# Spreading the DRAM weight sums of a hybrid encoder over the program: one transfer every 11 ticks, group by group

## The chip, the cores and the metric

One core of a Trainium2 chip runs one program. The metric is the device time of one execution in microseconds (us). The engines are TensorE (PE, with its weight loads PEld), VectorE (DVE), ScalarE (ACT), GpSimd (POOL) and SyncE (SP). DMA transfers are issued from SP's, ACT's and POOL's queues and moved by 16 DMA engines. All data are float32.

## The reference, cut to what matters

One layer over 2048 positions of width 1024. It is a mixer with two branches followed by a gated feed-forward network:

```python
xn = rmsnorm(x, norm1_g)
z = xn @ w_in                                   # 1024 -> 4608 columns
u_pool, zq, zf, zi, zo, zg = split(z)
gates = sigmoid(zg + b_gate)                    # two branches of 1024
ya = pool_mixer(u_pool, pool_w, pool_scale) @ w_pa     # trailing means, windows 2, 4, 8, 16
yb = hgrn2_mixer(zq, zf, zi, zo, lb, norm_g) @ w_pb    # gated recurrence, 4 heads
x = x + (gates[0] * ya + gates[1] * yb) @ w_o
h = causal_conv3(rmsnorm(x, norm2_g) @ w_up) + conv_b  # 1024 -> 5632
val, gate = split(h)
x = x + (silu(gate) * val) @ w_down                    # 2816 -> 1024
out = rmsnorm(x, final_g)
```

## The kernel before, in words

**Passes and stages.** The program runs twice over its weights, each time for two blocks of 512 positions (1024 in all). Each pass has these stages: `io` (the recurrence's input and output-gate columns), the projection (14 units of the other columns of `w_in`), the two branch products `pa` and `pb`, the output projection `wo`, the up-projection `up` (22 units with convolution and gate) and the down-projection `dn`.

**Seven products in place of eight.** The large products use a Strassen-type scheme (Winograd's form). A 2 by 2 block product is made of seven block products, called P1 to P7 here (M1 to M7 for `wo` and `dn`), for which sums of weight blocks and sums of input blocks are needed. For a pair of weight tiles with four quarters, the four sums are s1, s2, s3 and s4: s1 = q2 + q3, s3 = q2 + q0, s2 = s1 + q0 and s4 = s2 + q1. P5 uses s1, P6 uses s2, P7 uses s3, P3 uses s4; P1, P2 and P4 use plain quarters.

**Two float32r halves.** Each operand is split into a high part (a cast on ACT, line 207 for weights) and a low part (a subtraction on DVE, line 208). Every block product is three matmuls: high by high, high by low, low by high.

**The weight stream.** The class `Stream` holds the whole program's list of weight operands in order. A raw tile of 128 by 512 is loaded through SP's queue (line 185) up to 8 tiles ahead (`N_RAW`), and an operand is converted up to 4 ahead of the one in use (`LOOKAHEAD`, 6 buffers).

**Ticks.** Every sixth matmul of the helper `mm` is a tick (`MM_PER_TICK = 6`). At a tick the stream converts at most one operand, and every live task is stepped whose wait, in ticks, is over. A unit of seven products has 84 matmuls, 14 ticks; one operand lasts two ticks. Matmuls of the recurrence aren't counted.

**Where the weight sums come from.** The up-projection's sums are made in DRAM and are used in both passes. The second pass takes those of `io` and of the projection from DRAM as well. The first pass makes its own `io` and projection sums as it goes, on POOL (lines 311 and 369; some of `io`'s on DVE). The sums in DRAM are made in groups of mostly four units: six groups for `up` (tiles `su0` to `su5`), one for `io` (`so0`) and four for the projection (`si0` to `si3`: the forget and query columns, gates 0 to 3, the pool columns with two units, gates 4 to 7). A group takes eight transfers, each of 1 MB (512 KB for a group of two): four plain copies issued on ACT (line 263) and four that add to what lies in DRAM, issued on POOL (line 260, `accum_op`). In each group the order is: s1 = q2, s3 = q2, s1 += q3, s3 += q0, s2 = s1, s2 += q0, s4 = s2, s4 += q1. That makes 11 groups, 88 transfers.

**When they are issued before.** `Sums.make` starts a task that issues one transfer and then waits `SUM_LAG = 4` ticks. It goes through the eight steps in the outer loop and through the groups in the inner one. The `up` task starts when the first `io` stage is done (line 1103): 48 transfers in 192 ticks. The `io` and projection tasks start together at the first up-projection (lines 1373 and 1374): 8 transfers in 32 ticks beside 32 in 128. A load that needs a sum finishes the whole task first (`join` in `of`).

**The scheduler's freedom.** The program is given to a scheduler that orders each engine's instructions by a simulated timeline. A copy on ACT is tied behind the stream's latest cast (`issue_after(stream.mark.ins)`), so it isn't placed ahead of the tick at which it is issued. An accumulation on POOL has no such tie, only its dependence on the transfer whose result it adds to.

The task's heart, lines 252 to 264:

```python
for dst, src, add in (("s1", 2, 0), ("s3", 2, 0), ("s1", 3, 1), ("s3", 0, 1),
                      ("s2", "s1", 0), ("s2", 0, 1), ("s4", "s2", 0), ("s4", 1, 1)):
    for g in range(n):
        ...
        yield SUM_LAG
```

Of the kernel before, what the change touches and what calls it, by code (L numbers as in the profile page):

```python
# [11 lines left out]
F32 = mybir.dt.float32  # L12
# [3 lines left out]
ALU = mybir.AluOpType  # L16
AX = mybir.AxisListType

P = 128
# [52 lines left out]
FIN_WAIT = 4  # L72
N_RAW = 8
GROUP = 4
SUM_LAG = 4
N_OPS = 6
LOOKAHEAD = 4
MM_PER_TICK = 6
# [3 lines left out]
def tile_trunk(  # L82
# [16 lines left out]
    pe, act, dve, pool, sp = nc.tensor, nc.scalar, nc.vector, nc.gpsimd, nc.sync  # L99
# [6 lines left out]
    dram = ctx.enter_context(tc.tile_pool(name="dram", bufs=1, space=bass.MemoryType.DRAM))  # L106
# [15 lines left out]
    class Task:  # L122
        def __init__(self, gen):
            self.gen = gen
            self.wait = 0
            self.live = True
            tasks.append(self)
# [15 lines left out]
    def join(task):  # L143
        while task.live:
            task.step()
# [86 lines left out]
    stream = Stream()  # L232

    class Sums:


        def __init__(self, name, groups):

            self.name, self.groups = name, groups
            self.where = {}  # L240
            self.task = None
            for g, (units, _) in enumerate(groups):
                for i, u in enumerate(units):
                    self.where[u] = g, i
            self.t = {}

        def make(self):
            def gen():
                n = len(self.groups)
                for g, (units, _) in enumerate(self.groups):  # L250
                    for k in ("s1", "s2", "s3", "s4"):
                        nm = f"{self.name}{g}{k}"
                        self.t[g, k] = dram.tile([P, len(units), 512], F32, tag=nm, name=nm)
                for dst, src, add in (("s1", 2, 0), ("s3", 2, 0), ("s1", 3, 1), ("s3", 0, 1),
                                      ("s2", "s1", 0), ("s2", 0, 1), ("s4", "s2", 0),
                                      ("s4", 1, 1)):
                    for g in range(n):
                        x = self.t[g, src] if isinstance(src, str) else self.groups[g][1][src]
                        if add:
                            pool.dma_start(self.t[g, dst], x, accum_op=ALU.add)  # L260
                        else:
                            with tc.issue_after(stream.mark.ins):
                                act.dma_start(self.t[g, dst], x)
                        yield SUM_LAG

            self.task = Task(gen())

        def of(self, unit, key):
            def src():
                join(self.task)  # L270
                g, i = self.where[unit]
                return self.t[g, key][:, i, :]
            return src

    def grouped(src, mv, mg, names):
        n = len(names)

        def part(m, c):
            m0, st = m[0], m[1] - m[0]
            v = src[m0 : m0 + st * (n - 1) + 1 : st].rearrange("m p c -> p m c")  # L280
            return v[:, :, c * 512 : (c + 1) * 512]

        return names, [part(mv, 0), part(mv, 1), part(mg, 0), part(mg, 1)]
# [54 lines left out]
    def proj_tiles(kind, i):  # L338
        if kind == "fq":
            return C_F // P + i, C_Q // P + i  # L340
        if kind == "u":
            return 2 * i, 2 * i + 1
        return C_G // P + i, C_G // P + KD + i
# [91 lines left out]
    sums = {}  # L435
# [6 lines left out]
    def group_in(kind, i0, n):  # L442
        mv, mg = zip(*(proj_tiles(kind, i) for i in range(i0, i0 + n + 1)))
        return grouped(w_in_t, mv, mg, [(kind, i) for i in range(i0, i0 + n)])

    io_q = w_io.rearrange("k p c -> p k c")
    sums["up"] = Sums("su", [group_up(m0) for m0 in range(0, MF, GROUP)])
    sums["io"] = Sums("so", [(list(range(4)),
                              [io_q[:, :, c * 512 : (c + 1) * 512] for c in (0, 3, 1, 2)])])
    sums["in"] = Sums("si", [group_in(*g) for g in (("fq", 0, 4), ("g", 0, 4), ("u", 0, 2),  # L450
                                                    ("g", 4, 4))])

# [642 lines left out]
    def mixer(b0, forms, late):  # L1095
# [4 lines left out]
        md, od, gd = {}, {}, {}  # L1100
        proj_io(b0, forms, late, vd, zd)
        if b0 == 0:
            sums["up"].make()


        queue = []
# [171 lines left out]
    def ffn(b0, forms, late):  # L1278
# [90 lines left out]
                gs[k, hf] = fetch(gd[k, hf], f"g{b0}_{k}_{hf}")  # L1369
            return gs[k, hf]  # L1370

        if not b0:
            sums["io"].make()
            sums["in"].make()
        down = Rows(f"dn{b0}", "dn", DOWN, MF // 2, get_g, acc, 5)
        EARLY = {"P7": 2, "P4": 3}
        units = {}
# [63 lines left out]
    for b in range(0, SEQ // TB, 2):  # L1441
        forms, task, late = nxt
        join(task)
        forms, task, late = mixer(b, forms, late)
        join(task)
        nxt = ffn(b, forms, late)
# [47 lines left out]
```

## Time and profile before

| what | value |
|---|---|
| time, median of 3 runs | 2718.53 us (2715.54 to 2718.91) |
| the profiled execution's own time | 2723.21 us |
| its span, first to last instruction | 2721.5 us |
| mean granted TensorE clock | 0.979 |
| busy share PE, DVE, ACT, POOL | 94%, 80%, 43%, 41% |
| moved by DMA | 467.50 MB, mean 172 GB/s |
| of these by POOL's queue (q0) | 41.95 MB, 21184 packets |
| of these by ACT's queue (q10) | 67.23 MB, 25264 packets |

How to read it: the page is one execution. A queue's bytes include reads and writes of stores and fetches that have nothing to do with sums, on ACT's queue above all. Busy time of an engine is given as a share of the span, or of a stretch where a row names one. A row of the chain of waits has its start, its length and what ran or was waited for. In rows of instructions, a line number is that of the kernel, then come the operation, output and inputs by the program's names with the buffer numbers left out, the count, and the time. A waiting row reads "engine, what waited, what it waited for: us in total, times, longest".

### The profile page before, as it was taken

The page shows a single profiled execution, that of the slowest core. Times are in us where ns is not written, and L with a number is a line of the kernel's source. Part 1 is how long each engine was busy: PE and PEld are TensorE (multiplying, and loading weights), DVE is VectorE, ACT ScalarE, POOL GpSimd, SP SyncE. Part 2 cuts the span into 40 slices and gives each one's busy share as a digit, 9 for nine tenths or more (in the row PEclk, how much of TensorE's full clock was granted, in tenths as well). Part 3 has the DMA queues.
Part 4 walks back from the last instruction along what each step waited for, and adds up shares of the span by engine and source line. Part 5 has one row for each costly group of instructions (what it writes and reads, how often), then busy time and mean ns, then how long its engine had stood idle before and what let it go on. Part 6 is the DMA issues. An engine that isn't in the chain of part 4 may idle for free.

```text
span 2721.5 us, 35290 instructions
## 1 busy us (share of the span) xinstructions
PE 2571.2 (94%) x11464; PEld 2072.5 (76%) x11464; DVE 2190.7 (80%) x3414; ACT 1166.9 (43%) x2204; POOL 1113.3 (41%) x1171
## 2 busy tenths in 40 slices
PE   7989998999799999989999999999999999998898
PEld 6777777887578888767878788888777888885686
DVE  7879779579687777799987777674898777778998
ACT  5324333423454444443364344342345544444344
POOL 5544344076442111197761111211853211117785
PEclk9999999999899999999999999999999999999999
DMA  6797569654999543474465344347443433436552
GB/s 213 216 265 194 153 192 236 212 192 153 284 262 284 165 127 118 143 262 132 159 198 159 97 124 128 113 150 246 164 146 94 126 121 123 121 123 227 196 168 85
DMA packets 254472, 467.50 MB, mean 172 GB/s; under 512 B 24688, under 2 KB 41200, under 8 KB 253936
## 3 DMA queue, kind: packets, MB, share of 16 engines
q1 hardware_dynamic: 207840, 356.08, 41.1%
q0 software_dynamic: 21184, 41.95, 8.7%
q10 hardware_dynamic: 25264, 67.23, 6.6%
q8 instruction: 90, 1.47, 0.2%
q14 instruction: 94, 0.77, 0.1%
HBM read 391.75 MB, written 157.29 MB: 202 GB/s over the span
## 4 chain that ended last, share of the span: by engine, by line
PE 60%; DVE 16%; DMA 7%; issue 5%; POOL 5%; ACT 2%; SPq 0%; ACTq 0%; DVEq 0%; POOLq 0%
PE up_Z L148 13%; PE up_X L148 8%; PE up_V L148 8%; DVE ops L208 5%; PE gr_Z L148 4%; PE pa L148 3%; PE pb L148 3%; PE gr_X L148 2%; PE gr_V L148 2%; PE dn_M L148 2%; PE fr_Z L148 2%; DMA g<-dg 1%; PE fr_X L148 1%; PE io_Z L148 1%; DMA su3s<-in_w_up_t 1%
## 5 line engine op out<-in xcount | busy, mean ns | idle before, releaser
L207 ACT CAST ops<-raw 128x512 fp32r<-128x512 f32 x582 | 358.5, 620 | 716.2 <-PE up_Z L148 240.0
L208 DVE TENSOR_TENSOR ops<-raw,ops 128x512 fp32r<-128x512 f32 x582 | 450.7, 780 | 124.1 <-ACT ops L207 119.1
L1296 POOL COPY hist<-h 128x2 f32<-128x2 f32 x88 | 38.3, 435 | 403.5 <-DVE h L942 402.9
L1301 DVE SCALAR_TENSOR_TENSOR e<-h,cols,e 128x512 f32<-128x512 f32 x176 | 136.3, 794 | 18.8 <-ACT e L1299 13.8
L1299 ACT ACTIVATE e<-h,cols 128x512 f32<-128x512 f32 x176 | 138.1, 812 | 19.0 <-DVE h L940 11.7
L1303 DVE SCALAR_TENSOR_TENSOR e<-h,cols,e 128x512 f32<-128x512 f32 x176 | 136.0, 777 | 1.3
L1294 POOL COPY h<-h 128x2 f32<-128x2 f32 x88 | 38.0, 458 | 152.1 <-DVE h L940 148.6
L1232 POOL TENSOR_TENSOR ya<-ya,gl 128x512 f32<-128x512 f32 x32 | 47.2, 1486 | 106.8 <-DVE gl L1231 106.8
L979 DVE TENSOR_TENSOR up_u<-up_Z,up_e 128x512 f32<-128x512 f32 x44 | 30.4, 690 | 66.8 <-PE up_Z L148 64.9
L1134 POOL TENSOR_TENSOR q<-q,qs 128x512 f32<-128x512 f32 x16 | 23.3, 1456 | 131.9 <-ACT qs L1133 94.1
L1307 ACT ACTIVATE e<-e 128x512 f32<-128x512 f32 x88 | 55.3, 629 | 40.6 <-DVE e L1303 40.6
L809 POOL COPY qm<-q 128x64 f32<-128x64 f32 x64 | 25.8, 457 | 109.5 <-DVE q L874 21.6
L1171 ACT ACTIVATE gt<-gt,cols 128x512 f32<-128x512 f32 x48 | 34.8, 726 | 74.0 <-DVE gt L942 58.0
L1038 DVE TENSOR_TENSOR ac<-ac,dn_M 128x512 f32<-128x512 f32 x96 | 59.9, 679 | 3.6 <-PE dn_M L148 3.6
L1038 DVE TENSOR_TENSOR x<-x,wo_M 128x512 f32<-128x512 f32 x96 | 61.1, 678 | 0.4
L940 DVE TENSOR_TENSOR h<-up_Z,up_e 128x512 f32<-128x512 f32 x44 | 30.4, 691 | 38.1 <-PE up_Z L148 38.0
L942 DVE TENSOR_TENSOR h<-up_u,up_V 128x512 f32<-128x512 f32 x88 | 60.0, 682 | 0.1
L817 PE MATMUL pl<-qm,k 128*128 128x192 f32 x256 | 48.7, 332 | 8.0 <-DVE f L835 3.1
L817 PEld LDWEIGHTS pl<-qm,k 128*128 128x128 f32 x256 | 43.1, 191 | 13.1 <-issue 4.6
L148 PE MATMUL dn_M<-ops,dn_M_0h 128*128 128x512 f32 x112 | 39.3, 425 | 13.9 <-DVE ops L208 5.5
L1294 POOL COPY h<-hist 128x2 f32<-128x2 f32 x88 | 52.2, 642 | 0.0
L1308 DVE TENSOR_TENSOR e<-e,e 128x512 f32<-128x512 f32 x72 | 51.6, 717 | 0.4
(1743 smaller groups left out, 9025.4 us busy)
## 6 DMA issues: line engine op xcount, KB each, us to landing
raw<-in_w_dn SPq DMA_DIRECT2D x198, 256.0 KB, 3.6
raw<-in_w_up_t SPq DMA_DIRECT2D x132, 256.0 KB, 3.2
raw<-in_w_in_t SPq DMA_DIRECT2D x98, 256.0 KB, 3.6
dg<-e SPq DMA_DIRECT2D x88, 256.0 KB, 3.5
g<-dg SPq DMA_DIRECT2D x88, 256.0 KB, 5.3
raw<-in_w_o SPq DMA_DIRECT2D x80, 256.0 KB, 3.6
raw<-in_w_io SPq DMA_DIRECT2D x68, 256.0 KB, 4.9
x<-in_x SPq DMA_DIRECT2D x64, 256.0 KB, 5.3
```

What stands on the lines that cost most here:

```text
L148: pe.matmul(*args, **kw)
L207: self.mark = act.copy(hi, v)
L208: dve.tensor_tensor(lo, v, f32(hi), ALU.subtract)
L817: pe.matmul(pa_[:, c * 192 : c * 192 + 192], ks[:, (i + c) * P : (i + c + 1) * P], mv[:, c].rearrange("p s x -> p (s x)"), start=True, sto ...
L942: dve.tensor_tensor(dst, t, ps, ALU.add if how == "add" else ALU.subtract)
L1038: dve.tensor_tensor(t, t, ps[pr[0], j], ALU.add if sg > 0 else ALU.subtract)
L1294: pool.tensor_copy(h[:, 0:2], hist[:, mt] if hf == 0 else hs[s, 0][:, TB : TB + 2])
L1299: act.activation(t, h[:, 2:], AF.Identity, bias=col(o_cb + mt), scale=col(o_cw + 4 * MF + mt))
L1301: dve.scalar_tensor_tensor(t, h[:, 1 : 1 + TB], col(o_cw + 2 * MF + mt), t, ALU.mult, ALU.add)
L1303: dve.scalar_tensor_tensor(t, h[:, 0:TB], col(o_cw + mt), t, ALU.mult, ALU.add)
L1307: act.activation(g, g, AF.Silu)
L1308: (pool if m < G_POOL else dve).tensor_tensor(g, g, ts[0, hf], ALU.mult)
```

## The change

One task makes all the sums, for `up`, then `io`, then the projection, group after group in the order in which they are used. Each group's eight transfers come one after another, 11 ticks apart (`SUM_LAG = 11`). The task starts where the `up` task started, after the first `io` stage. A load that needs a sum steps the task until that sum's group is done, rather than finishing all of it. The number of transfers, their sizes, their engines and what they compute stay.

```diff
-SUM_LAG = 4
+SUM_LAG = 11
...
-            self.task = None
+            self.done = set()
...
-        def make(self):
-            def gen():
-                n = len(self.groups)
...
-                    for g in range(n):
-                        x = self.t[g, src] if isinstance(src, str) else self.groups[g][1][src]
...
-            self.task = Task(gen())
+        def make(self, g):
+            n = len(self.groups[g][0])
+            for k in ("s1", "s2", "s3", "s4"):
+                nm = f"{self.name}{g}{k}"
+                self.t[g, k] = dram.tile([P, n, 512], F32, tag=nm, name=nm)
+            for dst, src, add in (("s1", 2, 0), ("s3", 2, 0), ("s1", 3, 1), ("s3", 0, 1),
+                                  ("s2", "s1", 0), ("s2", 0, 1), ("s4", "s2", 0), ("s4", 1, 1)):
+                x = self.t[g, src] if isinstance(src, str) else self.groups[g][1][src]
+                if add:
+                    pool.dma_start(self.t[g, dst], x, accum_op=ALU.add)
+                else:
+                    with tc.issue_after(stream.mark.ins):
+                        act.dma_start(self.t[g, dst], x)
+                yield SUM_LAG
+            self.done.add(g)
 
         def of(self, unit, key):
             def src():
-                join(self.task)
                 g, i = self.where[unit]
+                while g not in self.done:
+                    prep[0].step()
                 return self.t[g, key][:, i, :]
...
+    prep = []
+
+    def prepare():
+        for name in ("up", "io", "in"):
+            for g in range(len(sums[name].groups)):
+                yield from sums[name].make(g)
...
         if b0 == 0:
-            sums["up"].make()
+            prep.append(Task(prepare()))
...
-        if not b0:
-            sums["io"].make()
-            sums["in"].make()
```

More of the change, by code (lines that the diff above doesn't have):

```diff
@@ L245, in __init__ @@
             self.t = {}
-        def make(self):
-            def gen():
-                n = len(self.groups)
[L250 to L256, printed above, removed]
-                    for g in range(n):
-                        x = self.t[g, src] if isinstance(src, str) else self.groups[g][1][src]
[L259 to L264, printed above, removed]
-            self.task = Task(gen())
+        def make(self, g):
[13 more added lines that the diff above has]
+            self.done.add(g)
         def of(self, unit, key):
             def src():
-                join(self.task)
                 g, i = self.where[unit]
+                while g not in self.done:
+                    prep[0].step()
                 return self.t[g, key][:, i, :]
```

## The prediction

> **What bounds the kernel now.** I read the page first, then the busy time by stage, then the chain of waits inside the two bursts.
>
> ```profile
> span 2721.5 us, 35290 instructions
> PE 2571.2 (94%) x11464; PEld 2072.5 (76%) x11464; DVE 2190.7 (80%) x3414; ACT 1166.9 (43%) x2204; POOL 1113.3 (41%) x1171
> 113.00:506.00 393.00, 362.06 (x1775) 297.81 (x1774) 311.51 (x686) 143.38 (x323) 153.18 (x165) 0.98 0.78 209
> 506.00:596.00 90.00, 90.00 (x397) 73.03 (x397) 52.00 (x76) 23.17 (x46) 33.27 (x24) 1.00 0.68 233
> 596.00:688.00 92.00, 85.83 (x371) 66.75 (x369) 90.41 (x106) 37.64 (x72) 64.58 (x52) 0.98 0.46 149
> 1155.00:1385.00 230.00, 215.29 (x888) 168.28 (x887) 227.61 (x206) 100.21 (x185) 190.66 (x134) 0.97 0.57 189
> 1489.00:1842.00 353.00, 349.57 (x1769) 293.12 (x1768) 259.04 (x669) 143.48 (x318) 55.14 (x86) 0.99 0.42 127
> ```
>
> A window row has its stretch and length, then busy time of PE, PEld, DVE, ACT and POOL, the granted clock, the DMA share and GB/s. TensorE is busy for 94% of the span: time can be won only where it waits. The kernel runs the same program twice over 1024 positions, and the second pass makes no weight sums, so it is a yardstick. The projection stage (113 to 506) takes 393 us in the first pass, 353 in the second.
>
> The second burst (40 transfers) starts with the up-projection. Rows of the chain for the fifth unit's start, and the first matmuls of that stage in the two passes:
>
> ```profile
> L148 PE MATMUL up_X<-m_f0h,ops x88: 388/397/474, 688.0 to 2435.2; 128*128 128x512 f32 x88
> 809.03 3.25 PE up_X L148 x14
> L148 PE MATMUL up_X<-m_f0h,ops x8: 392/394/474, 2024.0 to 2032.8; 128*128 128x512 f32 x8
> 2123.93 3.24 PE up_X L148 x14
> ```
>
> From 688.0 to 809.03 is 121.0 us, from 2024.0 to 2123.93 it is 99.9: the same work loses **21.1 us** beside the burst. What the loss is made of, from the chain, the timeline of ACT's queue and the waits:
>
> ```profile
> 697.70 28.31 DMA si2s<-in_w_in_t
> 712.83 0.51 ACTq L263 DMA_DIRECT2D so0s<-so0s  x1
> 726.02 0.55 ACTq L263 DMA_DIRECT2D si0s<-in_w_in_t  x1
> 726.62 0.62 ACT L561 CAST m_T21h<-m_t 128x512 fp32r<-128x512 f32 x1 [13.13 <-DMA si2s<-in_w_in_t]
> PE up_Z L148 <- ACT m_T21h L561: 11.6, 1, 11.6
> ```
>
> A copy issued at 697.70 landed 28.31 us later; the next issue on ACT's queue stood behind it until 726.02, ACT's casts behind that, and TensorE waited 11.6 us for one of them.
>
> **The change, part by part.** All 88 transfers stay (44 copies issued on ACT, 44 accumulations on POOL, mostly 1 MB). Only times of issue move. A tick is six matmuls, a unit of seven products 14 ticks, so the stages start at these ticks: projection 56, branches 252, output projection 316, up 372, down 680, second io 834, second projection 890. Before, 48 transfers go 4 ticks apart from tick 57 and 40 in two tasks from 372. The rows of one group check the clockwork:
>
> ```profile
> L263 ACTq DMA_DIRECT2D su0s<-in_w_up_t x2: 577/624/671, 116.2 to 167.1; - x2
> L263 ACTq DMA_DIRECT2D su0s<-su0s x2: 533/1147/1761, 310.1 to 404.6; - x2
> L260 POOL DMA_DIRECT2D su0s<-in_w_up_t x4: 1169/1259/1431, 122.5 to 412.7; - x4
> ```
>
> Six groups lie 24 ticks apart: 167.1 - 116.2 is 2.12 us a tick, (404.6 - 310.1) / 48 is 1.97. POOL's first accumulation is due at tick 105, near 213 us, yet starts at 122.5: accumulations are placed earlier, right behind their copy; copies keep their tick.
>
> After, transfer i goes at tick 57 + 11 i: 18 in the projection, 6 in the branches, 5 in the output projection, 28 in up, 14 in down (7 of them accumulations), 5 in the second io, 12 later. A group takes 88 ticks. Demand: sums are loaded up to 24 ticks ahead of use (8 loads and 4 operands of 2 ticks), so the up groups are wanted from 370, 406, 462, 518, 574 and 630 and are there at 145, 233, 321, 409, 497, 585; io is wanted at 826 (there 673), the first two groups of the input projection at 868 and 882 (761, 849). The third (u) is wanted near 896 and due at 937: its last three transfers are forced out together.
>
> *First up stage.* Of the 40, 24 were issued between 676 and 800 for 21.1 us, 0.88 each. Five remain in the stage's first 58 ticks: between 0 and 4.4 us stay. I take 2: **-19**.
>
> *First projection.* Stretches with and without transfers:
>
> ```profile
> 113.00:250.00 137.00, 122.11 (x581) 98.89 (x580) 105.25 (x221) 47.44 (x106) 60.05 (x63) 0.98 0.99 256
> 250.00:300.00 50.00, 48.15 (x236) 39.11 (x236) 42.26 (x113) 18.22 (x36) 12.74 (x16) 1.00 0.28 96
> 300.00:360.00 60.00, 55.37 (x279) 46.58 (x278) 45.79 (x114) 21.19 (x56) 25.60 (x28) 0.97 0.86 234
> 360.00:400.00 40.00, 38.39 (x208) 31.82 (x206) 29.81 (x63) 12.77 (x29) 21.18 (x25) 1.00 0.44 107
> 400.00:470.00 70.00, 64.33 (x297) 53.28 (x297) 64.42 (x127) 26.96 (x60) 29.87 (x32) 0.95 0.97 256
> 470.00:500.00 30.00, 27.71 (x152) 23.01 (x151) 20.98 (x49) 13.63 (x27) 2.50 (x2) 1.00 0.46 144
> POOL su3s L260 <- DMA su3s<-in_w_up_t: 18.2, 2, 11.8
> ACT ops L207 <- POOL w51s L369: 7.4, 1, 7.4
>   DMA su3s<-su3s: 5.7, 1
> ```
>
> In 267 us with transfers TensorE idles 25.2; in 120 without, 5.8, which is 12.8 for 267. So 12.4 us are theirs by idle time. By matmuls done (1157 in 267 against 596 in 120) it would be 34, but the early stretch has fewer of the short ones, so that is an upper end. The way is shown: POOL stands in front of an accumulation up to 11.8 us, the weight sum behind it is late, ACT's cast waits 7.4 (the last row is POOL's stand for a copy in the calmer second part of the burst). With 18 of 48 left, 12.4 x 30/48 = 7.8 goes at least; I take **-10** (up to -34).
>
> *Branches, rest of up, second io and projection.* **0**. Cover: TensorE is busy 90.00 of 90 us in the branches at a DMA share of 0.68, and 349.57 of 353 in the second projection at 0.42. In the up stage it holds even with the second half of the burst beside it (the DMA rows give queue, count, KB each and median us to landing over the whole run):
>
> ```profile
> 850.00:900.00 50.00, 50.00 (x218) 40.59 (x217) 36.60 (x57) 23.73 (x39) 10.29 (x18) 1.00 1.05 286
> si2s<-si2s ACTq DMA_DIRECT2D x2, 512.0 KB, 8.1
> si2s<-in_w_in_t POOLq DMA_DIRECT2D x4, 512.0 KB, 19.8
> raw<-si2s SPq DMA_DIRECT2D x8, 256.0 KB, 2.7
> ```
>
> The forced group u costs at worst its chain, 8.1 + 19.8 + 2.7 = 31 us, against 24 ticks of 1.80 us (353 / 196), 43 us. SP's loads and fetches behind it are late by as much and still in time; without that lead 31 us would be lost.
>
> *Output projection.* Two accumulations where DVE is full (90.41 of 92): 2 x 1.16 at most; a gain is excluded, as nothing leaves that stage. I take **+2**.
>
> *Down stage.* New there: seven accumulations and seven copies. The trace of before has none in this stage. POOL is nearly full where it begins and then the path runs through fetches:
>
> ```profile
> L260 POOL DMA_DIRECT2D si3s<-in_w_in_t x4: 1160/1163/1192, 735.9 to 880.1; - x4
> 1150.00:1200.00 50.00, 42.43 (x162) 31.69 (x163) 47.99 (x38) 23.71 (x40) 44.86 (x31) 0.93 0.75 248
> 1188.61 6.98 DMA g<-dg
> 1195.65 5.13 DMA raw<-in_w_dn
> 1200.85 5.21 DMA g<-dg
> 1206.12 4.65 DMA g<-dg
> ```
>
> Each accumulation holds POOL for 1.16 us: 8.1 for seven, if POOL is the path throughout. Lower end 0 (POOL has 39 of 230 us free; nothing here can get faster, as no transfer leaves this stage). Upper end: each also stands for its copy, 5.7 us as in the calmer part of the first burst: 7 x 6.9 = 48. A full POOL can't take them early, so the copy will have landed; I take **+8**.
>
> Sum: -19 - 10 + 2 + 8 = **-19**. The profiled execution took 2723.21 us, 1.7 around its span of 2721.5, so it would take 2704.2; it lies 4.7 above the median of the runs, 2718.53. For the median: **2699.5**.
>
> **The rivals.**
>
> *More is won (R1).* The projection gives back all 34, the up stage all 21, the rest as forecast: -45, 2673.5. For it: the chain between 125 and 215 runs mostly through those landings. Against: the matmul mix, and DVE's 311.51 busy of 393.
>
> *The projection gives nothing (R2).* The same wait stands before every accumulation that is placed right behind its copy; eight of them at 5.7 are 46 us of POOL's standing. Then -19 + 10 = -9, 2709.5.
>
> *Shared bandwidth in the down stage (R3).* Two copies and two accumulations are due at ticks 673 to 706, which is about 1145 to 1195 us, beside the four fetches quoted (22.0 us of chain). These rows say what a load costs with the sums in flight and without, from 676 to 800 and from 950 to 1050:
>
> ```profile
> raw<-in_w_up_t SPq DMA_DIRECT2D x11, 256.0 KB, 9.5
> raw<-in_w_up_t SPq DMA_DIRECT2D x16, 256.0 KB, 3.0
> ```
>
> With two queues where the burst had three, a load would take about twice its 3.0 us, so the 22.0 us of links could become 44: -19 + 22 is +3; with half of the links hit, -8. I put it at the middle, -2: 2716.5. Against: the wait is one stretch, and later loads are far ahead. The Trainium skill, "DMA: Bandwidth & Descriptors", section "Queues, rings and completion order", says that each DMA engine takes the queues that have work in turn, a packet from each; the ratio 9.5 to 3.0 with three queues at work agrees, and by it two queues give the factor 2. It speaks against moving transfers from a stage with cover to one whose chain runs through loads.
>
> *Slower: POOL stands in the down stage (R4).* The scheduler places the seven accumulations right behind their copies there too, and POOL waits 5.7 us for each with its own sums for the down product queued behind, for which ACT and TensorE wait. 7 x 6.9 = 48 instead of 8: -19 + 40 = +21, 2739.5. It decides from 27 / 7 = 3.9 us of unhidden standing per accumulation on. For it: POOL's 44.86 of 50; against: 39 us free in the stage.
>
> *The change doesn't even them out (R5).* Only copies are tied to a tick; if accumulations and loads are placed so that bursts come back, or the forced group stops SP beyond its 43 us, gains and losses cancel: 2718.5.
>
> **How the numbers follow.** Forecast 0.48 (its own range 2690 to 2709), R1 0.12, R2 0.12, R3 0.08, R4 0.12, R5 0.08. Leaving out R4 and the far half of R1: 2682 to 2722. About 0.2% (5.4 us) is what a measurement of this kernel tells from no change. Faster by more: forecast, R1, and R2 less a little, 0.71; within: R3, R5 and that rest, 0.17; slower: R4, 0.12.
>
> **What would show it.** Right: the two copies of the first group's first sums near 116 and 139 us, the next two near 208 and 252; the fifth up unit about 102 us after the first, no cast of ACT waiting over 5 us there; the projection 380 to 385 us; loads in both places near 3 to 6 us instead of 9; accumulations in the down stage of 1.2 us with no wait on a copy. Wrong: a down stage longer by over 10 us, with POOL standing before accumulations; a projection still of 390; TensorE waiting for loads of the u sums behind the second io.

## The result, and the profile after

The change makes the kernel slower. The changed kernel takes **2732.86 us** (median of 4 runs, 2730.11 to 2735.8) against 2717.03 for the kernel before on the same chip: a ratio of **1.0061**, 95% interval 1.0043 to 1.0079. The forecast was 2699.5 (2682 to 2722).

The profiled execution took 2731.37 us, 8.2 more than that of before; by the medians it is 15.8, since the profile of before lies above its median and that of after below. Stages are read off the first matmuls. First those of the kernel before, then of the changed one (the first number behind the durations is the start; some rows cover both passes):

```profile
L148 PE MATMUL fr_X<-x_f0h,ops x16: 388/396/497, 113.2 to 1744.7; 128*128 128x512 f32 x16
L148 PE MATMUL wo_M<-ops,wo_M_0h x112: 387/393/508, 596.2 to 2009.8; 128*128 128x512 f32 x112
L148 PE MATMUL dn_M<-ops,dn_M_0h x112: 387/395/796, 1156.0 to 2683.2; 128*128 128x512 f32 x112
L148 PE MATMUL io_X<-ops,x_f0h x8: 392/396/477, 1407.3 to 1411.1; 128*128 128x512 f32 x8
```

```profile
L148 PE MATMUL fr_X<-x_f0h,ops x16: 393/398/503, 114.5 to 1752.6; 128*128 128x512 f32 x16
L148 PE MATMUL wo_M<-ops,wo_M_0h x112: 386/394/796, 585.9 to 2018.7; 128*128 128x512 f32 x112
L148 PE MATMUL up_X<-m_f0h,ops x88: 387/392/502, 688.7 to 2442.0; 128*128 128x512 f32 x88
L148 PE MATMUL dn_M<-ops,dn_M_0h x112: 386/397/797, 1139.1 to 2691.4; 128*128 128x512 f32 x112
L148 PE MATMUL io_X<-ops,x_f0h x8: 391/392/477, 1415.0 to 1421.4; 128*128 128x512 f32 x8
```

| stage of the first pass | before, us | after, us | difference | forecast |
|---|---|---|---|---|
| projection and branches | 483.0 | 471.4 | -11.6 | -10 |
| output projection | 91.8 | 102.8 | **+11.0** | +2 |
| up | 468.0 | 450.4 | -17.6 | -19 |
| down | 251.4 | 276.0 | **+24.6** | +8 |

The second pass begins 7.7 us later (1415.0 against 1407.3) and takes as long as before. So both gains came about as forecast, and two stages took back more than that: 35.6 us where the forecast had 10. The two stages by window, first before, then after (the columns are those of the window rows in the prediction):

```profile
1156.00:1407.00 251.00, 230.69 (x954) 179.24 (x953) 243.06 (x231) 113.86 (x220) 203.49 (x157) 0.97 0.58 191
```

```profile
586.00:688.00 102.00, 87.00 (x369) 68.03 (x367) 95.97 (x107) 37.60 (x72) 62.63 (x57) 0.92 0.60 172
1139.00:1415.00 276.00, 239.03 (x956) 186.06 (x956) 249.42 (x234) 115.80 (x220) 204.80 (x165) 0.91 0.77 233
```

TensorE does the same matmuls in each. In the down stage they keep it busy 8.3 us longer (239.03 against 230.69), at a granted clock of 0.91 against 0.97. Waits are followed by slow matmuls: behind the one that ends at 611.63 us in the output projection, single matmuls take 0.63 to 0.79 us, where 0.39 is usual. In the output projection VectorE's busy time grew from 90.41 to 95.97 us for about the same 106 instructions: some take longer. Its timeline names them (start, length, then the instruction); POOL's for the same stretch stands below it, and at the end the rows of the chain of waits that hold the two long ones:

```profile
598.25 10.23 DVE L565 TENSOR_TENSOR wo_M_1l<-wo_M_1s,wo_M_1h 128x512 fp32r<-128x512 f32 x1
608.40 0.68 DVE L565 TENSOR_TENSOR wo_M_1l<-ya,wo_M_1h 128x512 fp32r<-128x512 f32 x1
620.38 10.92 DVE L208 TENSOR_TENSOR ops<-w153b,ops 128x512 fp32r<-128x512 f32 x1
```

```profile
593.12 1.74 POOL L1013 TENSOR_TENSOR wo_M_0s<-ya,ya 128x512 f32<-128x512 f32 x1
594.82 1.76 POOL L1013 TENSOR_TENSOR wo_M_1s<-ya,ya 128x512 f32<-128x512 f32 x1
597.98 1.15 POOL L256 DMA_DIRECT2D su3s<-in_w_up_t  x1 [1.40 <-DMA su3s<-in_w_up_t]
598.64 1.79 POOL L1013 TENSOR_TENSOR wo_M_2s<-ya,ya 128x512 f32<-128x512 f32 x1
599.91 1.77 POOL L1013 TENSOR_TENSOR wo_M_3s<-ya,ya 128x512 f32<-128x512 f32 x1
...
606.17 1.75 POOL L426 TENSOR_TENSOR w155b<-raw,raw 128x512 f32<-128x512 f32 x1
```

```profile
598.33 2.82 DVE wo_M_1l L565
601.15 7.25 issue
...
620.47 10.84 DVE ops L208
```

A subtraction on VectorE that takes 0.68 us takes 10.23. It begins 0.27 us after POOL's DMA instruction does (597.98) and ends when POOL's run of seven sums is done (607.9). Ahead of the DMA POOL's sums start 1.70 us apart; behind it 1.25 us apart, each still recorded as 1.75 long, so they overlap. The down stage has five more such instructions (6.20, 10.26, 9.15, 6.33 and 6.50 us), each within 3 us behind an accumulation. The seven sum to 59.6 us. The kernel before issues no transfer in these two stages and has none there. Its two bursts have one over 5 us each, though. The longer, in the up stage, begins 1 us behind the start of an accumulation (735.85) and stands in the chain of waits as well, and that trace was at hand for the prediction:

```profile
736.84 5.88 DVE L562 TENSOR_TENSOR m_T10l<-m_t,m_T10h 128x512 fp32r<-128x512 f32 x1 [0.31 <-ACT m_T10h L561]
```

In the changed kernel's chain of waits through the two stages none of the nine accumulations has a row of its own, while long VectorE instructions do. Two rows of it from the down stage:

```profile
1215.30 10.18 DVE dn_M_0l L565
1296.91 6.33 DVE dn_M_3l L565
```

There is a second candidate in the down stage: POOL stands before accumulations, 32.9 us before its seven. Waits of POOL there:

```profile
POOL si1s L256 <- DMA si1s<-si1s: 11.9, 2, 9.1
POOL si0s L256 <- DMA si0s<-si0s: 11.1, 2, 6.3
POOL si1s L256 <- DMA si1s<-in_w_in_t: 9.3, 2, 7.3
```

So the theories are: **A**, the DMA instruction on POOL lets the run of sums behind it keep VectorE out (called the lock below); **B**, bandwidth, the traffic itself; and **S**, POOL's standing, which is the prediction's R4.

### The profile page after: what moved, and what is told of

Its sections match the earlier page's. It is cut to its first block, busy times and chain, and to the rows that moved or that the text cites. A ratio compares the mean times of both kernels' runs of the same rounds, so it can differ in the third digit from the quotient of the medians.

```text
span 2729.7 us, 35287 instructions
## 1 busy us (share of the span) xinstructions
PE 2578.0 (94%) x11464; PEld 2077.9 (76%) x11464; DVE 2194.1 (80%) x3414; ACT 1167.9 (43%) x2204; POOL 1100.4 (40%) x1171
## 4 chain that ended last, share of the span: by engine, by line
PE 65%; DVE 15%; DMA 6%; issue 4%; POOL 3%; ACT 2%; SPq 0%; ACTq 0%; DVEq 0%; POOLq 0%
PE up_Z L148 12%; PE up_X L148 9%; PE up_V L148 8%; PE dn_M L148 7%; DVE ops L208 4%; PE gr_Z L148 3%; PE pa L148 3%; PE pb L148 2%; PE gr_X L148 2%; PE fr_Z L148 2%; PE gr_V L148 2%; PE fr_X L148 1%; PE fr_V L148 1%; DMA g<-dg 1%; PE io_Z L148 1%
## 5 line engine op out<-in xcount | busy, mean ns | idle before, releaser
L208 DVE TENSOR_TENSOR ops<-raw,ops 128x512 fp32r<-128x512 f32 x582 | 445.0, 769 | 128.7 <-ACT ops L207 122.1
L148 PEld LDWEIGHTS dn_M<-ops,dn_M_0h 128*128 128x128 f32 x112 | 23.0, 209 | 40.3 <-DVE ac L1041 21.1
```

Of the source, the lines that this page charges most:

```text
L148: pe.matmul(*args, **kw)
L208: dve.tensor_tensor(lo, v, f32(hi), ALU.subtract)
```

## The experiments

Each is the changed kernel with the edit shown, except for two small kernels of phases. A variable `stage`, set at the start of each stage, tells the issuing code where it is.

**No accumulation in the two stages.** The nine accumulations issued there become copies on ACT's queue: as many transfers land, but POOL issues no DMA and doesn't stand. (The sums made there hold only their last term.)

```diff
-                if add:
+                if add and stage[0] not in ("wo", "dn"):
                     pool.dma_start(self.t[g, dst], x, accum_op=ALU.add)
```

> The changed kernel, but the nine accumulations issued while the output projection or the down stage of the first pass is being programmed (two of su3, four of si0, three of si1) go out as plain copies on ACT's queue. Those sums then hold only their last term. The bytes on the DMA engines stay nearly the same, POOL's DMA instructions in these stages are gone. The stages are measured from the first matmul of one to the first of the next: output projection 91.8 us before, 102.8 changed; down stage 251.3 before, 275.9 changed. Theory A (a DMA instruction on POOL lets the run of POOL sums behind it keep DVE's two-input instructions out; seven DVE instructions of 6.2 to 10.9 us, 59.6 in all, stand in these two stages): no DVE instruction over 3 us there, output projection 91 to 95, down stage 250 to 258, the median about 2695. Theory B (the 1 MB transfers take bandwidth from the loads): output projection over 99, down stage over 268, the median within 5 us of the changed kernel's 2732.9.

Measured: 2702.88 us, ratio 0.9936 (0.9923 to 0.9949), 8 us above theory A's figure. Output projection 93.5, down 257.6, up 447.0, projection and branches 469.6; no long VectorE instruction in the two stages. Against the kernel before, the traffic alone leaves +1.7 and +6.2. The rest, 9.3 and 18.4 us, hangs on the accumulations. The same two stages of the second pass, which no edit touches, scatter from 91.8 to 93.1 and from 248.2 to 251.8 us over these traces, so the 1.7 hardly stands out. The granted clock of the down stage is back at 0.96, TensorE's busy time at 231.73: the slow matmuls went with the waits.

**Tiny accumulations.** The nine stay on POOL but add 16 of 512 columns.

```diff
+                if add and stage[0] in ("wo", "dn"):
+                    pool.dma_start(self.t[g, dst][:, :, :16], x[:, :, :16], accum_op=ALU.add)
-                if add:
+                elif add:
```

> The changed kernel, but the same nine accumulations add only the first 16 of 512 columns: POOL's DMA instruction stays, its bytes are 1/32. Those sums are then incomplete. Theory A: the long DVE instructions stay (five or more over 5 us in the two stages), output projection 99 to 106, down stage 268 to 280, the median within 5 us of 2732.9. Theory B: output projection 91 to 95, down stage 250 to 260, the median under 2710.

Measured: 2731.1 us, ratio 1.0039 (1.0025 to 1.0052); output projection 103.8, down 275.2. One row of VectorE's timeline there:

```profile
1220.32 10.42 DVE L568 TENSOR_TENSOR dn_M_0l<-dn_M_0s,dn_M_0h 128x512 fp32r<-128x512 f32 x1
```

With a thirty-second of the bytes the loss stays, so the accumulations' bandwidth is not the cause. Both A and S survive, since POOL still waits for the copies here (37.4 us in the down stage).

**The lock by itself.** Two small kernels of phases, one execution each: VectorE makes ten additions (twenty where a phase of the second kernel has a wait) of 128x512 with both inputs in SBUF while POOL makes ten of the same, with or without a DMA instruction ahead of POOL's.

> The disputed cost by itself; none of the reference's layers is computed. In each phase DVE and POOL each start ten additions of 128x512 with two SBUF inputs at the same time, the phases one after the other. Phase a (after a warm-up phase w): no DMA ahead. b: an accumulating 1 MB DMA on POOL ahead of POOL's run. c: a plain 1 MB DMA on POOL ahead. d: no DMA, POOL runs memsets. f: accumulating DMA ahead, DVE's instructions have one SBUF input. g: accumulating DMA ahead, but after its third addition POOL waits for ACT. i: accumulating DMA ahead, POOL's run has four additions. Theory A: in a the engines take turns, every DVE instruction under 2 us, POOL's starts about 1.7 us apart; in b and c one DVE instruction lasts until POOL's run is over (10 x 1.25 = 12 us less what ran before it, 9 to 13 us) with POOL's starts 1.25 us apart; d and f have none over 2 us; g has one of 2 to 6 us; i one of 3 to 5 us. Theory B (bandwidth): no DVE instruction over 2 us in any phase, and b and c like a.

Rows of VectorE by phase (count: shortest/median/longest in ns), then the same ten as one stretch of its timeline:

```profile
L69 DVE TENSOR_TENSOR a_d<-c,a_g x10: 684/1745/1751, 24.7 to 37.6; 128x512 f32<-128x512 f32 x10
L69 DVE TENSOR_TENSOR b_d<-c,b_g x10: 678/679/13526, 44.4 to 62.7; 128x512 f32<-128x512 f32 x10
L69 DVE TENSOR_TENSOR d_d<-c,d_g x10: 684/684/692, 87.4 to 92.8; 128x512 f32<-128x512 f32 x10
L67 DVE TENSOR_SCALAR f_d<-f_g x10: 414/414/13371, 96.3 to 112.3; 128x512 f32<-128x512 f32 x10
```

```profile
24.72 14.64 DVE L69 TENSOR_TENSOR a_d<-c,a_g 128x512 f32<-128x512 f32 x10 [0.68 <-ACT a_g L44]
44.45 18.95 DVE L69 TENSOR_TENSOR b_d<-c,b_g 128x512 f32<-128x512 f32 x10 [0.68 <-ACT b_g L44]
```

Without a DMA (a) the engines take turns, 1.75 us each. Behind an accumulation (b) or a plain transfer (c, 12.98) one addition of VectorE stands 13 us, POOL's whole run; beside memsets of POOL (d) nothing stands. With four sums in POOL's run (phase i) the longest is 6.09, above the 3 to 5 expected. Two parts missed outright: a one-input operation on VectorE (f) stands just as long, and in phase g the gap I had put in POOL's run never left POOL idle, so it showed nothing. And the ten end only 4.3 us later in b than in a (18.95 against 14.64), since the other nine then run freely at 0.68: a long record overstates the loss.

> The port by itself again, with waits in POOL's run; none of the reference's layers is computed. Phases a and b as before (no DMA; accumulating DMA ahead of ten additions). c: DMA ahead, POOL's first addition waits about 8 us for a chain of ACT copies. f: DMA ahead, the fourth addition waits for such a chain. g: no DMA, the fourth addition waits. i: no DMA, a 512-column memset, a 2-column copy and another memset ahead of the run. DVE has twenty additions in c, f and g, ten otherwise. Theory A1 (the DMA lets POOL's next instruction be handed over before the one in front of it has ended, and that lasts until POOL runs empty): a and g take turns, no DVE instruction over 2 us; b one of 13 us; c none over 2 us, as POOL runs empty right behind the DMA; f one of 4 us, then turns; i like a. Theory A2 (a DMA gives POOL the port for a fixed time or for good): c and f show a DVE instruction of over 7 us behind the wait. Theory A3 (any quick POOL instruction ahead does it): i shows one of over 8 us.

```profile
L69 DVE TENSOR_TENSOR c_d<-c,c_g x20: 679/681/691, 65.8 to 77.3; 128x512 f32<-128x512 f32 x20
L67 POOL TENSOR_TENSOR c_p<-b,c_z x1: 4107/4107/4107, 75.0 to 75.0; 128x512 f32<-128x512 f32 x1
L69 DVE TENSOR_TENSOR f_d<-c,f_g x20: 677/680/4890, 92.8 to 115.9; 128x512 f32<-128x512 f32 x20
```

If POOL's first sum waits some 8 us behind the DMA (c), VectorE never stands; POOL's sum then stands 4.11 us for VectorE's own unbroken run. If the fourth sum waits (f), VectorE stands 4.89 us, until POOL's first three are done, and turns follow. A memset in the DMA's place (i) gives turns, 1.75 us at most; phase a gives turns and phase b a stand of 13.5 us, as in the first kernel. So a run behind a DMA keeps VectorE out until POOL is empty. The mirror case is seen in c alone: in f and g the fourth sum comes into a VectorE run that is going as well, and there it takes 1.62 and 1.26 us and turns follow. In c, POOL's sum is the first behind the DMA; whether that makes the difference, and why a DMA sets the lock going at all, was not tested. The 1.25 us between starts isn't the DMA's doing either: in c, once VectorE has finished, POOL's sums start 1.22 us apart.

The Trainium skill, "SBUF — State Buffer", section "Who interferes with whom", says that VectorE and GpSimd share a port pair as an exclusive lock which the first to issue holds for the whole instruction, that a VectorE operation with two SBUF inputs contends with a GpSimd one that reads SBUF and not with one that only writes, and lists `tensor_scalar` among those that can contend. Phases a, d and f agree (1.75, 0.68 and 13.37 us). Phase b doesn't: VectorE stands there for ten of POOL's instructions, 13.5 us, and not for one; what was measured decides.

**Breaking the run.** Behind each of the 44 accumulations, not only the nine, POOL must wait for a tiny copy on VectorE.

```diff
-                    pool.dma_start(self.t[g, dst], x, accum_op=ALU.add)
...
+                    d = pool.dma_start(self.t[g, dst], x, accum_op=ALU.add)
+                    with tc.issue_after(d.ins):
+                        z = pool.memset(gap[0], 0.0)
+                    dve.tensor_copy(gap[1], gap[0])
+                    with tc.issue_after(z.ins):
+                        pool.tensor_copy(gap[2], gap[1])
```

> The changed kernel with its transfers where they are; behind each accumulation POOL does a tiny memset, DVE copies that, and POOL copies DVE's result, so that POOL has to wait for DVE within a few instructions of the DMA. It computes the whole reference. Theory A1: no DVE instruction over 5 us in the output projection and the down stage (the run with POOL's accumulations replaced had none over 3), output projection 93 to 98, down stage 256 to 264, the median 2700 to 2714. If the long DVE instructions come from something else in these stages, they stay: down stage over 268, the median within 5 us of the changed kernel's.

Measured: 2737.6 us, ratio 1.0075 (1.0057 to 1.0094). The output projection is cured (94.7), the down stage is not (275.2, a miss), though its long VectorE instructions shrink to 3.8 us and less. Waits there:

```profile
POOL gap2si0s L263 <- DVE gap1si0s L261: 14.1, 3, 9.1
ACT dn_M_2h L571 <- POOL dn_M_2s L1020: 13.9, 4, 10.3
POOL gap2si1s L263 <- DVE gap1si1s L261: 11.3, 3, 9.7
```

POOL now waits 25.4 us for the tiny copies in VectorE's queue, and ACT for POOL's sums: one stall was swapped for another. The up stage, whose accumulations got the waits too, takes 456.9 instead of 450.4, and the median lies above the changed kernel's, where 2700 to 2714 was expected. In the output projection the two DMA instructions are still there, so its cure speaks for the lock and against POOL's time in the instruction itself. This tells nothing between A and S in the down stage.

**Standing and DMA taken apart.** Two runs split them. In the first, the nine accumulations are queued behind POOL's newest sum rather than right behind their copies, so that the copies have landed; everything is computed.

```diff
+                if add and stage[0] in ("wo", "dn"):
+                    with tc.issue_after(last[0].ins):
+                        pool.dma_start(self.t[g, dst], x, accum_op=ALU.add)
-                if add:
+                elif add:
...
-                pool.tensor_tensor(t, view(terms[0][0]), view(terms[1][0]), op)
+                last[0] = pool.tensor_tensor(t, view(terms[0][0]), view(terms[1][0]), op)
```

> The changed kernel with its nine accumulations of the output projection and the down stage queued behind the newest sum of POOL instead of right behind their copies; everything is computed. POOL then comes to them when the copy has long landed: its standing for copies, 32.9 us before the seven of the down stage, goes, and the DMA instructions stay. Theory A (the DMA instruction lets POOL's run of sums lock VectorE out): the long VectorE instructions of 6 to 11 us stay, the down stage 270 to 277 us (it took 276.0), the output projection 101 to 104. Theory S (what costs is POOL's standing, the sums behind it come late): down stage 256 to 262. Both in halves: 263 to 269. Time by A 2728 to 2734 us, by S 2712 to 2720.

In the second, each becomes a 128x1 copy on POOL that waits for a one-column load issued behind the accumulation's copy on ACT's queue.

```diff
+                if add and stage[0] in ("wo", "dn"):
+                    pool.tensor_copy(gap, self.seen[g, dst])
-                if add:
+                elif add:
...
                         act.dma_start(self.t[g, dst], x)
+                        if (self.name, g) in (("su", 3), ("si", 0), ("si", 1)):
...
+                            act.dma_start(seen, self.groups[g][1][1][:, 0, 0:1])
```

> The reverse: each of the nine accumulations of the output projection and the down stage becomes, at the same place in POOL's order, a copy of 128x1 on POOL that waits for a small load (one column) issued on ACT's queue right behind the accumulation's own copy; so POOL stands there about as long as before, but issues no DMA. The sums made there hold only their last term. Theory A: no VectorE instruction over 4 us in the two stages, down stage 255 to 261 us, output projection 93 to 95. Theory S: down stage 268 to 277, with POOL's waits of some 20 to 35 us in it. Both in halves: 262 to 267.

| nine accumulations of the two stages | POOL stands | DMA on POOL | us against before, run beside it | output projection | down |
|---|---|---|---|---|---|
| copies on ACT | no | no | -17.7 | 93.5 | 257.6 |
| waits without DMA | yes | no | -10.1 (ratio 0.9964, 0.995 to 0.9977) | 93.4 | 267.4 |
| queued late | no | yes | +4.2 (ratio 1.0014, 1.0003 to 1.0024) | 99.1 | 273.6 |
| the change | yes | yes | +15.8 | 102.8 | 276.0 |

A row of VectorE in the late-queued kernel, where POOL's longest wait for a copy was 2.9 us, and two waits of POOL in the other:

```profile
1185.82 8.72 DVE L570 TENSOR_TENSOR dn_M_7l<-dn_M_7s,dn_M_7h 128x512 fp32r<-128x512 f32 x1
```

```profile
POOL gapsi1s L258 <- DMA seensi1s2s<-in_w_in_t: 11.7, 1, 11.7
POOL gapsi0s L258 <- DMA seensi0s2s<-in_w_in_t: 9.5, 1, 9.5
```

Standing alone costs 7.6 us by the medians (9.7 in the two stages), the DMA instructions alone 21.9 (21.6), both 33.5 (27.7). So the DMA instructions are the larger part, two thirds by the medians and more by the stages, and standing a real smaller one, in the down stage only.

Neither theory's forecast came whole: queued late, the down stage lies in A's range and the output projection 2 us under it, with four VectorE instructions of 5.0 to 8.7 us left in the down stage and one of 8.6 in the output projection, but the time of 2722.35 lies between A's and S's; with waits alone no VectorE instruction is over 4 us, and the down stage's 267.4 lies at the upper edge of "both in halves".

In the down stage the two don't add up: 16.0 for the DMA instructions and 9.8 for the waits, 18.4 for both. And of the 16.0 no run takes POOL's own seven times 1.16 us, 8.1, apart from the lock; that none of them stands in the chain of waits, here or in the changed kernel, speaks against it. The stage lengths of the two split runs come from executions that were the slowest of their kernels' (2729.44 and 2718.28), which is why the medians stand first.

**Where else the transfers could go.** Three placements that compute everything. In the first, four groups go at distance 8 in the projection and branches, none until the up stage, and seven at distance 5 there.

```diff
-SUM_LAG = 11
+SUM_LAG = 8, 5
+N_FIRST = 4
...
+                while (name, g) == ("up", N_FIRST) and stage[0] != "up":
+                    yield 1
```

> All of the change's work, but no transfer in the output projection or the down stage: the first four groups go out 8 ticks apart in the projection and the branches, the task then waits for the up stage and sends the other seven groups 5 ticks apart. It computes the whole reference. Theory A: output projection 91 to 95, down stage 250 to 257, up stage 450 to 456 (changed 450.4, before 468.0), projection with branches 470 to 480 (changed 471.4, before 483.0); the median 2685 to 2702, faster than both. Theory B: the denser transfers in the up stage and the projection give back most of the 29 us won there; the median 2705 to 2720.

Measured: 2720.07 us, ratio 1.0000 (0.9987 to 1.0012). Output projection 94.7 and down 250.0 are cured, but the up stage takes 465.8, as the rival theory had it. (The stage lengths come from the fastest of the twelve executions, 2710.3 us, so they don't add up to the median.) From 850 to 1100 us, first this kernel with two rows of its chain of waits, then the last placement below:

```profile
850.00:1100.00 250.00, 242.87 (x1035) 194.58 (x1034) 177.43 (x271) 115.12 (x185) 42.89 (x91) 0.99 0.91 242
```

```profile
903.13 10.65 DMA si0s<-in_w_in_t
...
929.54 12.38 DMA si1s<-in_w_in_t
```

```profile
850.00:1100.00 250.00, 248.14 (x1066) 200.94 (x1065) 182.90 (x278) 117.30 (x188) 38.49 (x88) 0.99 0.82 218
```

At distance 5 the sums' own transfers enter the chain, and the up stage loses nearly all that the change had won there. In the second placement the groups go by stage:

```diff
-SUM_LAG = 11
+SUM_LAG = 6, 8, 7, 11
+N_FIRST = 5
+UP_LATE = 24
```

> All of the change's work, placed by stage: five groups 6 ticks apart in the projection and the branches, none in the output projection and the first 24 ticks of the up stage, four groups 8 ticks apart in the rest of the up stage, none in the down stage, the last two (7 and 11 ticks apart) in the second pass's io and projection. It computes the whole reference. Theory A: projection with branches 470 to 478, output projection 91 to 95, up stage 447 to 456 (the run with 5 ticks there had 465.8), down stage 249 to 254, and the median 2690 to 2704, 0.6 to 1.0% faster than before. If bandwidth is what the transfers cost wherever they lie, the median is 2710 to 2720, as in the run with the pause.

Five groups at 6 in the first stretch, four at 8 in the up stage (from its 24th tick), two in the second pass: 2728.68 us, ratio 1.0046 (1.0032 to 1.006). Output projection 94.3, up 451.1 and down 253.3 came as expected; projection and branches took 495.6, where 470 to 478 was expected, and the median lies above both theories' ranges. POOL stands up to 17.1 us before accumulations up to 490 us, and in the branches behind that up to 25.6 (second row, from 490 to 611 us); this run doesn't separate that from the rest.

```profile
POOL su3s L258 <- DMA su3s<-su3s: 17.1, 1, 17.1
POOL su4s L258 <- DMA su4s<-su4s: 42.9, 2, 25.6
```

The last takes the distances that had held (the edit is against the second placement):

```diff
-SUM_LAG = 6, 8, 7, 11
-N_FIRST = 5
+SUM_LAG = 8, 7, 7, 11
+N_FIRST = 4
```

> The stages again, with the distances that held in the runs so far: four groups at 8 units' distance in the first projection and branches (that stretch took 471.8 us so, and 495.6 with five groups at 6), nothing in the output projection and in the first 24 ticks of the up stage, then five groups at 7 in the up stage, nothing in the down stage, and the last two groups at 7 and 11 in the second input-output stage and projection, as before. Theory A (an accumulation costs where POOL's sums follow it in a run and VectorE is the bound, so in the output projection and the down stage, and nowhere else): projection and branches 468 to 475, output projection 94 to 95, up 450 to 458, down 250 to 254; against the kernel before (483.0, 91.8, 468.0, 251.4) that is 20 to 30 us less, 2687 to 2700 us as a median. Theory B (the sum of the traffic costs, wherever it lies): what the down stage and the output projection are spared comes back in the up stage and the second projection, and the time is that of the evenly spread kernel, 2725 to 2735. Between the two: the up stage above 462, as it was at a distance of 5 (465.8), and 2705 to 2715.

Measured: **2712.88 us, ratio 0.9976 (0.9963 to 0.9988)**, the one version that computes everything and is faster than the kernel before, by 6.8 us. The four stages came at the edges of theory A's ranges or 1 us beyond (475.3, 94.7, 449.5, 255.1), 19.6 us less than in the profile of before. The time is 13 us above the range that I had made of them, and in the one set for a case between the theories. In its profile the projection starts 6.5 us later (119.7 against 113.2 us) and all that follows the down stage takes 3.1 us longer (1317.3 against 1314.2), though no transfer was moved there but the last two groups; that was not followed up.

## Why the prediction was wrong, step by step

**Right, with sizes.** First up stage: forecast -19, measured -17.6; the fifth unit starts 101.8 us after the first (688.69 to 790.48, forecast 102), and ACT's longest wait in that stretch is 4.2 us. Loads took 3.1 us there and in the projection, where they had taken 9.5 and 6.6. First issues of group 0's copies, and these rows:

```profile
L259 ACTq DMA_DIRECT2D su0s<-in_w_up_t x2: 561/616/672, 117.5 to 138.7; - x2
L259 ACTq DMA_DIRECT2D su0s<-su0s x2: 500/514/529, 196.5 to 242.3; - x2
688.69 9.96 PE up_X L148 x42
790.48 3.25 PE up_X L148 x14
ACT ops L207 <- PE up_Z L148: 17.0, 8, 4.2
```

The clockwork held to 12 us (forecast 116, 139, 208 and 252). Projection: forecast -10, measured -11.6 with the branches; since the -10 was picked between 7.8 and 34, its nearness is partly luck. The projection stage by itself took 357.9, not 380 to 385, because the branch products began earlier among its last matmuls and took 23.6 longer; only the sum of the two can be read. The forced group u cost nothing: the second input-output stage took 81.5 us against 81.6.

**Wrong: output projection, +2.** The step was "two accumulations where DVE is full: 2 x 1.16 at most". It priced an instruction by the time it holds its own engine. Measured +11.0, of which 1.7 is traffic and 9.3 hangs on the accumulations; standing alone costs nothing there (93.4 against 93.5), and with the run behind each DMA instruction broken the stage takes 94.7, so it is the lock. The row that should have warned stood in the prediction: VectorE busy 90.41 of 92 us, with POOL's sums in the same stretch.

**Wrong: down stage, +8.** The step was "each accumulation holds POOL for 1.16 us: 8.1 for seven", with its second half "a full POOL can't take them early, so the copy will have landed". Both halves failed. The copies had not landed: POOL stood 32.9 us, which by the run with waits alone costs about 8 to 10. And the DMA instructions cost more than their hold of 8.1: with the standing gone, the stage still takes 273.6, 16.0 above the 257.6 of the kernel without them; the lock is the best account of it. The traffic cost 6.2, for which the forecast had nothing.

**The rivals.** R4 named the place, the sign and the smaller part of the mechanism. That its 2739.5 lies 7 us from the median is luck: POOL stood 4.7 us before each accumulation (32.9 / 7), near R4's 5.7, but R4 put all 40 us of standing on the path, four to five times the 7.6 to 9.7 that standing alone costs, and the larger part was in no rival. R3's shared bandwidth exists in the down stage (6.2 us, not 22). R1, R2 and R5 are out: the gains were neither larger nor missing. The forecast's two gains, -29, and the 7.9 us of traffic make -21; the kernel without these accumulations shows -20.6 by the profiles (2702.58 against 2723.21) and -17.7 by the medians.

**Two slips in the working.** The 3.9 us at which R4 was to decide is 27 / 7, an accumulation's whole cost at which the gains are used up; without the 1.16 us of its own it is 2.7 us of standing. And on ACT's queue two issues (709.64 and 712.83 us) went out while the copy of 697.70 was on its way, so it was the one after them that stood until 726.02, not the next. Neither changes the forecast.

## What to carry to other kernels

A DMA issued from POOL can cost more than its own 1.2 us. Look at what POOL runs behind it: where a run of POOL's SBUF reads follows at once and VectorE is the stage's bound, VectorE can stand for that whole run, so put such transfers where POOL's queue runs empty or where VectorE has slack. And before spreading work evenly over a program, price it stage by stage: even distances carried transfers out of stages with slack into the two that had none.

## What the runs showed of the hardware that was not expected

- Behind a DMA instruction on POOL, accumulating or plain, POOL's SBUF-reading sums start 1.25 us apart, as if alone, instead of 1.70, and one VectorE instruction stands for the whole run: 6.09 us for four sums, 13.5 for ten, 10.9 at most in the kernel. If POOL waits some 8 us between the DMA and its first sum, no VectorE instruction stands (0.69 us at most).
- Once, in phase c of the second small kernel, a VectorE run that was already going held POOL's sum for 4.11 us; in phases f and g it didn't (1.62 and 1.26).
- A one-input `tensor_scalar` of 128x512 in float32 stands as well, 13.37 us where it takes 0.41.
- The bytes of the transfer made no difference: with 16 of 512 columns the longest was 10.9 us.
- A stalled TensorE came back slower: the granted clock of the down stage fell from 0.97 to 0.91, and its matmuls took 8.3 us more.
